# A decoder layer on one core: the token sums' tiles start at another byte, and the first round of the gates spreads its seven products over more units

## The chip, the cores and the metric

The kernel runs on one core of a Trainium2 chip. The metric is the time of one launch on the device in microseconds (us); lower is better. A profile is one execution taken by the hardware profiler, and its trace can be asked for every instruction.

Engines are called by the profile's names: PE multiplies matrices (PEld is its loading of the stationary operand), DVE, ACT and POOL work on vectors, SP issues most of the transfers from memory.

## The reference, cut to what matters

One layer of a hybrid decoder works on 272 tokens (16 meta tokens and 256 others) of width 2048, all in float32:

```
proj = rmsnorm(h) @ w_in                 # one combined input projection
o_fox = forgetting_attention(...)        # 8 heads of 128
o_gla = gated_linear_attention(...)      # 4 heads, keys of 256, values of 512
y = sigmoid(gate_fox) * (o_fox @ w_o_fox) + sigmoid(gate_gla) * (o_gla @ w_o_gla)
h = h + y @ w_out
h = h + square(relu(rmsnorm(h) @ w_ff1)) @ w_ff2      # inner width 8192
out = rmsnorm(h)[:, 16:]
```

What bears on this case are the two gates' projections (`gate_fox`, `gate_gla`, each 2048 by 2048) with the branches' output projections, and the two matrices of the last sublayer.

## The kernel before, in words

**Precision.** A float32 operand is cut into two parts of a shorter type: ACT casts it to the high part (line 991 in `cut`), DVE subtracts that from the original to get the low part (line 992). A product of two cut operands is three matmuls on PE: high by high, high by low, low by high (`product_into`, line 1005). The stationary operand is a block of 128 by 128 numbers of the activations (tokens by inner dimension), the moving operand a row of 512 weights, so each of these matmuls streams 512 columns.

**Units.** A weight transfer of 512 KB fills a tile `raw` (five buffers), its cut fills a tile `w` (five buffers) that holds two blocks of the inner dimension for 512 columns. One such unit feeds twelve matmuls: two halves of the tokens (t = 0, 1), two blocks, three parts.

**Pairs with seven products.** The gates and the last sublayer are computed by `pair_of`: two column blocks f1 and f2 at a time, both token halves. For the first four blocks of the inner dimension it does not do the eight products of a 2 by 2 block product but seven (a scheme of Strassen's kind). For that it needs sums and differences of weights, which DVE makes from `hb`, `hc` and the raw tiles (line 996, `less`), and sums of token blocks, made once for each operand by `token_sums`. Four of the seven products take such a sum as the stationary operand (`summed(0)` to `summed(3)`). The seven products are step1 to step7; `held`, ahead of them, only issues the transfers of `hb` and `hc`. Step1 ends with a copy of bank x to bank y on ACT (line 1050), step2 with a copy of bank v to `m5` (line 1057). Step3 ends with z = x + m5 on DVE (line 1063), step4 with v = x + m5 (line 1067): the banks x, y, z, v are accumulators, so step4's product into x has to come behind the first of these additions, and any other product into x behind the second. The other twelve blocks of the inner dimension follow as plain units (six for each of the two column blocks).

**The rounds.** `columns` (heading of the code below: the function that the second part of the change touches) runs three rounds of the gates' pairs (b = 0, 1, 2). The list `work` has 24 units a round: eight `lone` units of the GLA branch's projection (tiles `gla<-w,og`), twelve plain units of the gates' pair (`bx`, `by`, `bz`, `bv` with `x` as the other operand), four `lone` units of the FoX branch's projection (`fox<-w,of`). A table `at` says behind which unit each of `held` and step1 to step7 is put. In the last sublayer thirteen pairs follow each other in the same way, seven with the operand x2 and six with the operand a, by a table of their own at the program's end; the four products with sums of each pair take their stationary operand from the tiles `s_x2` and `s_a`. (The profile leaves buffer numbers out of names: `x2` reads as `x` and `s_x2` as `s_x` there. Before 776 us `s_x` is the gates' own tile of sums, later it is `s_x2`.)

A scheduler that works on an estimated timeline places the instructions of each engine, so an instruction can end up some places before or behind where the code has it. `tc.keep_in_program_order` fixes `less` in its place.

**Where the operands begin.** Tiles of cut operands carry some spare columns, so that the code can choose the byte at which the operand begins (`at=24`, `at=56`, `SX_AT`, `SUMS_AT`; units of four bytes). The addresses in a partition, as the built program has them:

| operand | used as | in | begins at byte | past a multiple of 64 | past a multiple of 256 |
|---|---|---|---|---|---|
| x (cut activations), og, of | stationary | gates | 36992, 74112, 178304 | 0 | 128 |
| s_x (sums for the gates) | stationary | gates | 19328 | 0 | 128 |
| w in the gates' rounds | moving | gates | 128704 and on | 0 | 192 |
| x2, a | stationary | last sublayer | 73984, 37120 | 0 | 0 |
| s_x2, s_a, before | stationary | last sublayer | 197920, 206368 | 32 | 32 |
| s_x2, s_a, after | stationary | last sublayer | 197888, 206336 | 0 | 0 |
| w in the last sublayer's pairs | moving | last sublayer | 128576 and on | 0 | 64 |

Blocks inside an operand lie whole multiples of 256 bytes apart.

Of the kernel before, what the change touches and what calls it, by code (L numbers as in the profile page):

```python
# [30 lines left out]
BIG = 3.0e38  # L31
RAW = 5
NL = 4
SUMS_AT = 32
SX_AT = 0
PARTS_AT = 56

# [36 lines left out]
def trunk(ctx: ExitStack, tc: tile.TileContext, hT, w_small, w_all, consts, w_alpha2, out):  # L74
# [3 lines left out]
    def nm(s):  # L78
        serial[0] += 1
        return f"{s}_{serial[0]}"  # L80
# [11 lines left out]
    def bank(pool, s):  # L92
        return pool.tile([P, 512], F32, tag="bank", name=nm(s))
# [7 lines left out]
    def issued():  # L101
        for e in list(waiting):
            e[0] -= 1
            if e[0] <= 0:
                waiting.remove(e)
                e[1]()
# [126 lines left out]
    def cells(ap):  # L233
        return ap.rearrange("p (j m) -> p j m", m=P)

    def turn(rows, then, both, far=None, slots=(10, 12, 14), reload=None):

        n = 4 * NT
        for t, r in enumerate(rows):
            nc.vector.transpose(both[:, 0:n].rearrange("p (i t j r) -> p t i j r", i=4, t=2, r=32)[:, t],  # L240
                                r().rearrange("p j (i s) -> p i j s", i=4, s=32))
        there = far or dram.tile([P, n], F32, tag="there", name=nm("there"), bufs=2)

        def away():
            for c in range(4):
                nc.scalar.dma_start(there.rearrange("(i s) (c e) -> c s i e", i=4, c=4)[c],
                                    both[32 * c : 32 * c + 32, 0:n].rearrange("s (i e) -> s i e", i=4))

        behind.append([slots[0], away])
        if reload:  # L250
            behind.append([slots[0], reload])
        if far is None:
            back = both[:, n:]
            behind.append([slots[1], lambda: nc.scalar.dma_start(back, there)])
            behind.append([slots[2], lambda: then(returned(back))])
# [717 lines left out]
    def fetched(c0, k0, hold=None, pairs=False):  # L973
        if hold:
            raw = hold_pool[0].tile([P, HK * P], F32, tag=hold, name=nm(hold))
        else:
            raw = wp.tile([P, HK * P], F32, tag="raw", name=nm("raw"), bufs=RAW)
        cols = slice(k0 * P, (k0 + 2) * P)
        if pairs:
            for c in range(2):  # L980
                nc.sync.dma_start(raw[:, HK * P // 2 * c : HK * P // 2 * (c + 1)].rearrange("p (h e) -> p h e", h=2),
                                  w_all[c0 + c].rearrange("p (h e) -> p h e", h=2)[:, :, cols])
            return raw
        nc.sync.dma_start(raw.rearrange("p (c k m) -> p c k m", k=2, m=P),
                          w_all[c0 : c0 + 4, :, cols].rearrange("c p (k m) -> p c k m", m=P))
        return raw

    def cut(raw, low=False):
        hi, lo = (t.rearrange("p k m -> p (k m)").rearrange("p (k c m) -> p k c m", k=2, m=P) for t in pair(low=low))
        r = raw.rearrange("p (c k m) -> p k c m", k=2, m=P)  # L990
        copied = nc.scalar.copy(hi, r).ins  # L991
        made(copied, nc.vector.tensor_tensor(lo, r, hi.bitcast(F32), op=ALU.subtract).ins, 1)  # L992
        return [t.rearrange("p k c m -> p k (c m)") for t in (hi, lo)]
# [6 lines left out]
    def product_into(ps, xs, w, start=False):  # L1000
        for k in range(2):
            hi, lo = w[0][:, k, :], w[1][:, k, :]
            xh, xl = xs(k, 0), xs(k, 1)
            for i, (l, r) in enumerate(((xh, hi), (xh, lo), (xl, hi))):
                nc.tensor.matmul(steps(ps), l, steps(r), start=start and k == 0 and i == 0, stop=False,  # L1005
                                 skip_group_check=True)

    def tokens(x, t, k0):
        return lambda k, o: x[:, k0 + k, o, P * t : P * t + P]
# [89 lines left out]
    def columns():  # L1099

        hold_pool[0] = mp
        waiting_rows, far, made_s = {}, [], {}

        def lone(b, which, k0):
            key = (which, b)
            if k0 == 0:
                waiting_rows[key] = [bank(pg if which == "gla" else px, which), bank(px, which)]
            src, c0 = (og, A0 + 14 * b) if which == "gla" else (of, A0 + 14 * b + 12)
            w = cut(fetched(c0, k0, pairs=which == "fox"), True)
            for t, ps in enumerate(waiting_rows[key]):  # L1110
                product_into(ps, tokens(src, t, k0), w, k0 == 0)
            if which == "fox" and k0 == 6:
                joined(b)

        def gated(b, f, pt):
            g = "gf"[f]
            u = made_s[b, g] = mp.tile([P, 2, 512], F32, tag="s" + g, name=nm("s" + g))
            for t, ps in enumerate(pt):
                nc.scalar.activation(u[:, t, :], ps, AF.Sigmoid, scale=r1[:, t : t + 1])
            if g == "g":  # L1120
                for t, ps in enumerate(waiting_rows["gla", b]):
                    nc.vector.tensor_tensor(u[:, t, :], ps, u[:, t, :], op=ALU.mult)

        def joined(b):
            sf, sg = made_s[b, "f"], made_s[b, "g"]
            for t, ps in enumerate(waiting_rows["fox", b]):
                nc.vector.tensor_tensor(sf[:, t, :], ps, sf[:, t, :], op=ALU.mult)
            for t in range(2):
                nc.vector.tensor_tensor(sf[:, t, :], sf[:, t, :], sg[:, t, :], op=ALU.add)
            far.append(dram.tile([P, 4 * NT], F32, tag="far", name=nm("far"), bufs=3))  # L1130
            turn([lambda t=t: cells(sf[:, t, :]) for t in range(2)], None, sg.rearrange("p t f -> p (t f)"),
                 far=far[b], slots=(8,))

        made_pairs = [pair_of(A0 + 14 * b + 4, x, s_x, lambda f, pt, b=b: gated(b, f, pt), True, low=True)
                      for b in range(3)]
        work = []
        for b in range(3):
            work += [lambda b=b, k=k: lone(b, "gla", k) for k in range(0, KT, 2)]
            work += made_pairs[b][1]
            work += [lambda b=b, k=k: lone(b, "fox", k) for k in range(0, KT // 2, 2)]  # L1140
        at = {}
        for n, i in enumerate((-1, 0, 2, 3, 4, 5, 6, 7)):
            at.setdefault(i, []).append(made_pairs[0][0][n])
        for b in (1, 2):
            for n, i in enumerate((-3, -2, 0, 2, 3, 4, 6, 7)):
                at.setdefault(24 * b + i, []).append(made_pairs[b][0][n])
        for run in at[-1]:
            run()
        for i, run in enumerate(work):
            run()  # L1150
            for step in at.get(i, []):
                step()
            issued()
        chunk[0] += 42
        backs = [mp.tile([P, 4 * NT], F32, tag=t, name=nm("back")) for t in ("ha", "hb", "hc")]
        for b in (0, 1):
            nc.scalar.dma_start(backs[b], far[b])
        behind.append([11, lambda: nc.scalar.dma_start(backs[2], far[2])])
        return backs

    backs = columns()
    residual[0] = keep.tile([P, KT, NA + 3], F32, tag="h", name="h2")

# [49 lines left out]
    def sums_tile(name):  # L1213
        t = fp.tile([P, 16 * P + 64], F32R, name=name)
        return t[:, SUMS_AT : SUMS_AT + 16 * P].rearrange("p (s k o m) -> p s k o m", k=2, o=2, m=P)

# [325 lines left out]
```

## Time and profile before

| | |
|---|---|
| Median of 3 runs | 1517.83 us (1517.62 to 1518.39) |
| The profiled execution | 1518.05 us |
| its span, first to last instruction | 1516.3 us |
| granted TensorE clock | 0.999 |
| PE busy | 1505.9 us (99%) |
| DVE busy | 1121.8 us (74%) |
| ACT busy | 852.1 us (56%) |
| gates' rounds (matmuls of line 1005) | 482 to 700 us |
| output projection | about 740 to 841 us |
| last sublayer's pairs | 841 to 1377 us, their first products with sums from 784 us on |
| products of the last pair in token rows (lines 224 to 226) | 1377 to 1398 us |

How to read it: matmuls are pipelined, each is shown with a duration of about 380 ns although the next begins after 220 ns, so that PE reads as busy almost always. What a matmul costs is the distance from its beginning to the next one's. The chain of waits shows that: it lists pieces in order of time with the time that each took from the end of the piece before it, and a piece of x12 over 2.64 us is twelve matmuls 220 ns apart. A row of a view by windows gives the count of instructions that touch the window, so it counts one that began ahead of its left edge.

### The profile page before, as it was taken

The page shows a single profiled execution, that of the slowest core. Times are in us where ns is not written, and L with a number is a line of the kernel's source. Part 1 is how long each engine was busy: PE and PEld are TensorE (multiplying, and loading weights), DVE is VectorE, ACT ScalarE, POOL GpSimd, SP SyncE. Part 2 cuts the span into 40 slices and gives each one's busy share as a digit, 9 for nine tenths or more (in the row PEclk, how much of TensorE's full clock was granted, in tenths as well). Part 3 has the DMA queues.
Part 4 walks back from the last instruction along what each step waited for, and adds up shares of the span by engine and source line. Part 5 has one row for each costly group of instructions (what it writes and reads, how often), then busy time and mean ns, then how long its engine had stood idle before and what let it go on. Part 6 is the DMA issues. An engine that isn't in the chain of part 4 may idle for free.

```text
span 1516.3 us, 22651 instructions
## 1 busy us (share of the span) xinstructions
PE 1505.9 (99%) x8518; PEld 1334.7 (88%) x8518; DVE 1121.8 (74%) x1508; ACT 852.1 (56%) x1223; POOL 129.5 (9%) x200
## 2 busy tenths in 40 slices
PE   9999999999999999999999999999999999999997
PEld 8999999999998888888988888888888888888997
DVE  7898858586676766756798887677877788875765
ACT  7766444555555554444566666556654566455563
POOL 6012110111111000000011000000000000100021
PEclk9999999999999999999999999999999999999999
DMA  9545545465555757586668588567775678787652
GB/s 319 177 146 187 178 159 192 156 211 174 169 185 182 230 185 236 184 291 212 217 212 263 168 282 258 196 198 249 251 236 196 214 244 259 250 292 253 228 201 86
DMA packets 224194, 323.10 MB, mean 213 GB/s; under 512 B 12154, under 2 KB 189316, under 8 KB 223956
## 3 DMA queue, kind: packets, MB, share of 16 engines
q1 hardware_dynamic: 203332, 292.40, 58.5%
q10 hardware_dynamic: 20496, 27.99, 6.0%
q8 instruction: 67, 1.10, 0.3%
q0 software_dynamic: 256, 1.26, 0.3%
q14 instruction: 43, 0.35, 0.1%
HBM read 305.86 MB, written 15.74 MB: 212 GB/s over the span
## 4 chain that ended last, share of the span: by engine, by line
PE 96%; DVE 2%; issue 1%; ACT 1%; POOL 0%; POOLq 0%; DVEq 0%
PE ps L191 16%; PE bx L1005 14%; PE bz L1005 10%; PE by L1005 10%; PE bv L1005 10%; PE ps L192 8%; PE psa L196 5%; PE psa L200 5%; PE psa L198 4%; PE gla L1005 4%; PE fox L1005 2%; PE ps L466 2%; PE ps L468 1%; PE ps L1409 1%; DVE w L135 1%
## 5 line engine op out<-in xcount | busy, mean ns | idle before, releaser
L992 DVE TENSOR_TENSOR w<-raw,w 128x1024 fp32r<-128x1024 f32 x260 | 319.8, 1231 | 152.7 <-ACT w L991 148.4
L991 ACT CAST w<-raw 128x1024 fp32r<-128x1024 f32 x260 | 271.3, 1048 | 218.6 <-PE bv L1005 86.2
L135 DVE TENSOR_TENSOR w<-raw,w 128x1024 fp32r<-128x1024 f32 x222 | 272.5, 1228 | 101.4 <-ACT w L134 97.8
L134 ACT CAST w<-raw 128x1024 fp32r<-128x1024 f32 x222 | 232.6, 1049 | 97.0 <-PE psa L200 30.7
L191 PE MATMUL ps<-x,w 128*128 128x512 f32 x607 | 206.0, 383 | 0.0
L196 PE MATMUL psa<-x,w 128*128 128x272 f32 x640 | 181.7, 285 | 0.0
L200 PE MATMUL psa<-x,w 128*128 128x272 f32 x640 | 179.7, 282 | 0.0
L198 PE MATMUL psa<-x,w 128*128 128x272 f32 x624 | 175.9, 282 | 0.0
L192 PE MATMUL ps<-x,w 128*128 128x256 f32 x607 | 166.6, 274 | 0.0
L191 PEld LDWEIGHTS ps<-x,w 128*128 128x128 f32 x607 | 113.9, 188 | 19.3
L196 PEld LDWEIGHTS psa<-x,w 128*128 128x128 f32 x640 | 120.2, 188 | 0.2
L200 PEld LDWEIGHTS psa<-x,w 128*128 128x128 f32 x640 | 120.2, 188 | 0.1
L1005 PE MATMUL bx<-w,x 128*128 128x512 f32 x480 | 120.1, 382 | 0.0
L198 PEld LDWEIGHTS psa<-x,w 128*128 128x128 f32 x624 | 117.4, 188 | 0.0
L192 PEld LDWEIGHTS ps<-x,w 128*128 128x128 f32 x607 | 114.0, 188 | 0.0
L1005 PE MATMUL by<-w,x 128*128 128x512 f32 x420 | 105.8, 382 | 0.0
L1005 PEld LDWEIGHTS bx<-w,x 128*128 128x128 f32 x480 | 89.8, 187 | 16.6
L1005 PE MATMUL bv<-w,x 128*128 128x512 f32 x360 | 91.6, 383 | 0.0
L1005 PEld LDWEIGHTS by<-w,x 128*128 128x128 f32 x420 | 78.7, 187 | 14.5
L1005 PE MATMUL bz<-w,x 128*128 128x512 f32 x360 | 91.4, 383 | 0.0
L191 PE MATMUL ps<-y,w 128*128 128x512 f32 x256 | 85.7, 380 | 0.0
L991 ACT CAST w<-ha 128x1024 fp32r<-128x1024 f32 x48 | 50.3, 1047 | 53.2 <-PE bx L1005 22.7
(405 smaller groups left out, 2776.1 us busy)
## 6 DMA issues: line engine op xcount, KB each, us to landing
raw<-w_all_dram SPq DMA_DIRECT2D x493, 512.0 KB, 4.3
there<-turn ACTq DMA_DIRECT2D x76, 128.0 KB, 4.2
turn<-there ACTq DMA_DIRECT2D x19, 512.0 KB, 5.5
hb<-w_all_dram SPq DMA_DIRECT2D x16, 512.0 KB, 4.3
hc<-w_all_dram SPq DMA_DIRECT2D x16, 512.0 KB, 5.9
raw<-w_all_dram SPq DMA_DIRECT2D x26, 256.0 KB, 3.4
raw<-w_all_dram SPq DMA_DIRECT2D x8, 384.0 KB, 6.5
h<-hT_dram SPq DMA_DIRECT2D x8, 275.0 KB, 6.8
```

Source lines behind the costliest of these rows:

```text
L134: copied = nc.scalar.copy(hi[:, k, :], r).ins
L135: return copied, nc.vector.tensor_tensor(lo[:, k, :], r, hi[:, k, :].bitcast(F32), op=ALU.subtract).ins
L191: nc.tensor.matmul(steps(ps), hi, steps(row(x)), start=first, stop=False)
L192: nc.tensor.matmul(steps(ps[:, 0:NT]), lo, steps(x[:, 0, :]), start=False, stop=last)
L196: nc.tensor.matmul(steps(ps[:, X_LO]), hi, steps(x_lo[:, k]), start=first, stop=False, skip_group_check=True)
L198: nc.tensor.matmul(steps(ps[:, 0:NA]), lo, steps(x_hi[:, k]), start=False, stop=last and hi is None, skip_group_check=True)
L200: nc.tensor.matmul(steps(ps[:, 0:NA]), hi, steps(x_hi[:, k]), start=False, stop=last, skip_group_check=True)
L466: nc.tensor.matmul(steps(ps), hi, steps(row(x[:, k])), start=st, stop=False)
L468: nc.tensor.matmul(steps(ps[:, 0:NT]), lo, steps(x[:, k, 0]), start=False, stop=sp)
L991: copied = nc.scalar.copy(hi, r).ins
L992: made(copied, nc.vector.tensor_tensor(lo, r, hi.bitcast(F32), op=ALU.subtract).ins, 1)
L1005: nc.tensor.matmul(steps(ps), l, steps(r), start=start and k == 0 and i == 0, stop=False, skip_group_check=True)
```

## The change

Two numbers change. The constant `SUMS_AT`, the place at which the sums' operand begins in the tiles `s_x2` and `s_a`, goes from 32 to 24 (32 bytes further to the front). And the table for the first round (b = 0) in `columns` is spread out: `held` stays ahead of the first unit, step1 to step7 come behind units 1, 3, 5, 7, 9, 10 and 12 instead of 0 and 2 to 7.

```
-SUMS_AT = 32
+SUMS_AT = 24
...
         at = {}
-        for n, i in enumerate((-1, 0, 2, 3, 4, 5, 6, 7)):
+        for n, i in enumerate((-1, 1, 3, 5, 7, 9, 10, 12)):
             at.setdefault(i, []).append(made_pairs[0][0][n])
```

The first number moves no instruction. The second does, in the first round alone. On PE, at the round's beginning, this stood before (gla and og are the GLA branch's accumulators and input, bx and bv the gates' accumulators, w a cut weight tile):

```order
L1005 MATMUL gla_5833<-w_5837,og_1382 128x4x32x4 x6
L1005 MATMUL gla_5834<-w_5837,og_1382 128x4x32x4 x6
L1005 MATMUL bx_5859<-w_5854,x 128x4x32x4 x6
L1005 MATMUL gla_5833<-w_5870,og_1382 128x4x32x4 x6
L1005 MATMUL gla_5834<-w_5870,og_1382 128x4x32x4 x6
L1005 MATMUL gla_5833<-w_5887,og_1382 128x4x32x4 x6
L1005 MATMUL gla_5834<-w_5887,og_1382 128x4x32x4 x6
L1005 MATMUL bv_5906<-w_5902,s_x 128x4x32x4 x6
```

and now stands this:

```order
L1005 MATMUL gla_5833<-w_5837,og_1382 128x4x32x4 x6
L1005 MATMUL gla_5834<-w_5837,og_1382 128x4x32x4 x6
L1005 MATMUL gla_5833<-w_5854,og_1382 128x4x32x4 x6
L1005 MATMUL gla_5834<-w_5854,og_1382 128x4x32x4 x6
L1005 MATMUL bx_5876<-w_5871,x 128x4x32x4 x6
L1005 MATMUL gla_5833<-w_5887,og_1382 128x4x32x4 x6
L1005 MATMUL gla_5834<-w_5887,og_1382 128x4x32x4 x6
L1005 MATMUL gla_5833<-w_5904,og_1382 128x4x32x4 x6
L1005 MATMUL gla_5834<-w_5904,og_1382 128x4x32x4 x6
L1005 MATMUL bv_5923<-w_5919,s_x 128x4x32x4 x6
```

Step1 (bx from x) and step2 (bv from s_x) each stand one or two GLA units later.

Where step4 and step5 stood on PE among the last GLA units (bx and bz from s_x), before:

```order
L1005 MATMUL gla_5833<-w_5999,og_1382 128x4x32x4
L1005 MATMUL gla_5834<-w_5999,og_1382 128x4x32x4
L1005 MATMUL bx_5859<-w_5961,s_x 128x4x32x4 x6
L1005 MATMUL bz_5942<-w_5988,s_x 128x4x32x4 x6
L1005 MATMUL gla_5833<-w_5999,og_1382 128x4x32x4 x5
L1005 MATMUL gla_5834<-w_5999,og_1382 128x4x32x4 x5
L1005 MATMUL by_5866<-w_6016,x 128x4x32x4 x6
```

they now stand among the first plain units (by and bx from x):

```order
L1005 MATMUL gla_5834<-w_5997,og_1382 128x4x32x4 x6
L1005 MATMUL by_5883<-w_6024,x 128x4x32x4 x3
L1005 MATMUL bx_5876<-w_6012,s_x 128x4x32x4 x6
L1005 MATMUL by_5883<-w_6024,x 128x4x32x4 x3
L1005 MATMUL by_5883<-w_6041,x 128x4x32x4 x6
L1005 MATMUL bz_5976<-w_6056,s_x 128x4x32x4 x6
L1005 MATMUL by_5883<-w_6067,x 128x4x32x4 x6
L1005 MATMUL bx_5876<-w_6024,x 128x4x32x4 x6
L1005 MATMUL bx_5876<-w_6041,x 128x4x32x4 x6
```

The scheduler has put the plain products into bx of three units behind three units' products into by, because the addition of step4 stands between them. On DVE, the two additions (lines 1063 and 1067) stood before among these cuts:

```order
L992 TENSOR_TENSOR w_5988<-hc_5831,w_5988 128x1024
L1063 TENSOR_TENSOR bz_5942<-bx_5859,m_821_5913 128x512
L992 TENSOR_TENSOR w_5999<-raw_5997,w_5999 128x1024
L992 TENSOR_TENSOR w_6016<-raw_6014,w_6016 128x1024
L996 TENSOR_TENSOR ha_5857<-raw_6014,ha_5857 128x1024
L992 TENSOR_TENSOR w_6028<-raw_6026,w_6028 128x1024
L1067 TENSOR_TENSOR bv_5906<-bx_5859,m_821_5913 128x512
L992 TENSOR_TENSOR w_6043<-ha_5857,w_6043 128x1024
```

and now among these:

```order
L992 TENSOR_TENSOR w_6024<-raw_6022,w_6024 128x1024
L1063 TENSOR_TENSOR bz_5976<-bx_5876,m_823_5930 128x512
L992 TENSOR_TENSOR w_6041<-raw_6039,w_6041 128x1024
L992 TENSOR_TENSOR w_6056<-hc_5831,w_6056 128x1024
L992 TENSOR_TENSOR w_6067<-raw_6065,w_6067 128x1024
L1067 TENSOR_TENSOR bv_5923<-bx_5876,m_823_5930 128x512
L992 TENSOR_TENSOR w_6084<-raw_6082,w_6084 128x1024
L996 TENSOR_TENSOR ha_5874<-raw_6082,ha_5874 128x1024
L992 TENSOR_TENSOR w_6096<-raw_6094,w_6096 128x1024
```

The first addition now stands behind the cut of the first plain unit, the second behind two more. Also on DVE, at the round's beginning, the first difference of weights (line 996, from `hb`) comes one place earlier: ahead of the eviction of the last gate of the stage before (line 287) and of the cut of `w_5904`, where it stood behind that eviction. On SP the transfers of the second round's `hb` and `hc` are issued some places later among those of the raw tiles. POOL's order is the same.

## The prediction

> **What bounds the kernel now.** I read the page first: its busy times and its chain of waits.
>
> ```profile
> span 1516.3 us, 22651 instructions
> PE 1505.9 (99%) x8518; PEld 1334.7 (88%) x8518; DVE 1121.8 (74%) x1508; ACT 852.1 (56%) x1223; POOL 129.5 (9%) x200
> PE 96%; DVE 2%; issue 1%; ACT 1%; POOL 0%; POOLq 0%; DVEq 0%
> ```
>
> PE is the bound from one end to the other. So the question for each half of the change is not who is busy, but whether PE waits anywhere that the change touches, and how far apart its matmuls begin. I therefore went to the chain in order of time, which gives that distance. First the gates' rounds, with pieces that take the sums as stationary operand (491.59) and pieces that don't:
>
> ```profile
> 482.35 2.64 PE gla L1005 x12
> 491.59 1.32 PE bv L1005 x6
> 544.39 7.92 PE fox L1005 x36
> ```
>
> Each is 0.220 us a matmul: 2.64/12, 1.32/6, 7.92/36. Now the last sublayer, from its first pair on:
>
> ```profile
> 841.73 1.32 PE bx L1005 x6
> 849.65 1.76 PE bx L1005 x8
> 855.38 0.89 PE by L1005 x4
> 856.27 1.35 PE bv L1005 x6
> 858.07 2.69 PE bx L1005 x12
> 894.38 2.68 PE bx L1005 x12
> 975.48 2.74 PE bx L1005 x12
> ```
>
> It also begins at 0.220 (1.32/6, 1.76/8). At 856.27 come six products with the sums `s_x2`: 0.225 each. After them the distance doesn't go back, although the operands are again x2 and plain weights: 0.223 at 894 (2.68/12), 0.228 at 975 (2.74/12). Over whole stages (PE's rows by windows; the gates' rounds, the pairs from the first sums at 856 on, and the last pair's token rows):
>
> ```profile
> 482.35:699.90 217.55, 217.55 (x991) 1.00 0.69 225
> 856.11:1376.98 520.87, 520.87 (x2319) 1.00 0.75 239
> 1376.98:1398.20 21.22, 21.22 (x96) 1.00 0.78 264
> ```
>
> The clock is 1.00 in all three. 217.55 us at 0.220 is 989 matmuls, which is the count but for the edge and two short ones at the left: no time is lost in the gates. 520.87 us for 2318 (one of the 2319 began earlier) is 0.2247 each: the last sublayer's pairs are 2% slower than the same instruction in the gates. That is not a wait for another engine, as PE's rows there show no idle time, and it is not the work beside it, since it begins with one group of products. The same group can be watched where it stands alone among the output projection's matmuls (512 and 256 columns in turn):
>
> ```profile
> 803.82 0.38 PE L191 MATMUL ps<-y,w 128*128 128x512 f32 x1
> 804.15 1.51 PE L1005 MATMUL bx<-w,s_x 128*128 128x512 f32 x6
> 805.51 0.38 PE L191 MATMUL ps<-y,w 128*128 128x512 f32 x1
> 806.86 0.38 PE L191 MATMUL ps<-y,w 128*128 128x512 f32 x1
> 808.19 0.38 PE L191 MATMUL ps<-y,w 128*128 128x512 f32 x1
> ```
>
> From 804.15 to 805.51 the six with sums take 1.36 us where six take 1.32 in the gates; the four pairs from 805.51 take 1.35, the next four 1.33. The disturbance comes with the sums and dies out here; among the pairs of the last sublayer it stays.
>
> **What sets the sums apart.** All stationary operands of the pairs, x2 and a, and all of the gates, begin at a multiple of 64 bytes; `s_x2` and `s_a` alone begin 32 bytes past one. The gates' own sums begin at a multiple and run at 0.220. So my theory is: while a matmul streams its moving operand, PE loads the next stationary block; these two streams run in step as long as their offsets agree, the 32 bytes put them out of step, and x2 and a can't bring them back.
>
> **Part one, SUMS_AT 32 to 24.** It adds and removes no instruction. After it `s_x2` and `s_a` begin at a multiple of 64, in fact of 256, as x2 and a do. If the step is kept, each of the 2318 matmuls costs what x2's cost at 841 to 850: 2318 x 0.220 = 510.0, against 520.87: -10.9 us. The last pair's token rows (95 that begin in the window, 0.2234 each) follow in the same state: 95 x 0.220 = 20.9 against 21.22, -0.3. The four groups with sums ahead of 856, of which the one at 804 is quoted, lose 1.36 - 1.32 = 0.04 each and 0.02 behind it: -0.2 in all. Sum -11.4. No row in these stages is below 0.220, so that is also the most that it can give.
>
> The least: only the sums' own products improve and x2 and a stay at the 0.2233 of the row at 894. Then 2318 x 0.2233 = 517.6: -3.2 us (less the token rows, which are there already). Below nothing: everything settles at the 0.2283 of the row at 975, 2318 x 0.2283 = 529.2, +8.4. I take the first value: x2 has run at 0.220 with exactly the addresses that all operands will have, and 72 products with aligned sums in the gates have not moved their neighbours.
>
> A rule speaks against this half. The Trainium skill, page "SBUF — State Buffer", section "Who interferes with whom", gives PE two independent read ports, one for the moving operand and one for the weight load, and says that PE never waits on anyone; by that rule the start byte would change nothing and part one would come to 0. The trace doesn't bear it out: the products at 856.27 and 491.59 differ in nothing that the profile shows but their operands, and take 1.35 and 1.32.
>
> Does another engine become late when PE is 2% faster? DVE is the nearest (columns: PE, PEld, DVE, ACT, POOL):
>
> ```profile
> 482.00:545.00 63.00, 63.00 (x289) 53.75 (x288) 41.01 (x37) 32.28 (x35) 0.73 (x1) 1.00 0.71 227
> 866.80:945.00 78.20, 78.20 (x351) 65.44 (x350) 64.42 (x66) 50.07 (x60) 0.00 (x0) 1.00 0.84 267
> ```
>
> In the densest stretch it works 64.4 of 78.2 us, 82%; with 1.5 to 2% less time, 84%. The stretch at 856 and on has PE without idle time at 82%, so I put this at 0, with 0.5 us as the bound for a few first waits.
>
> **Part two, the first round's table.** It moves step1 to step7 behind later units; the same matmuls, cuts, differences and transfers are issued. What it could remove is PE's waiting in that round, up to its first FoX product:
>
> ```profile
> 482.35:544.39 62.04, 62.04 (x284) 1.00 0.71 227
> ```
>
> There is none: 282 matmuls (two of the 284 began earlier) at 0.220 are 62.04. So its gain is bounded at 0. What it could add hangs on three places.
>
> ```profile
> L1063 DVE TENSOR_TENSOR bz<-bx,m 128x512 f32<-128x512 f32 x16 | 11.1, 694 | 3.1 <-PE bx L1005 3.1
> L1067 DVE TENSOR_TENSOR bv<-bx,m 128x512 f32<-128x512 f32 x16 | 11.1, 694 | 1.7 <-PE bx L1005 1.7
> L992 DVE TENSOR_TENSOR w<-raw,w 128x1024 fp32r<-128x1024 f32 x260 | 319.8, 1231 | 152.7 <-ACT w L991 148.4
> L991 ACT CAST w<-raw 128x1024 fp32r<-128x1024 f32 x260 | 271.3, 1048 | 218.6 <-PE bv L1005 86.2
> L287 DVE TENSOR_TENSOR evt<-ps,evb 128x256 f32<-128x256 f32 x5 | 2.1, 423 | 2.1 <-ACT evb L284 2.1
> L996 DVE TENSOR_TENSOR ha<-hb,raw 128x1024 f32<-128x1024 f32 x1 | 1.2, 1226 | 1.3 <-DMA hb<-w_all_dram 1.3
> ```
>
> First, step4's product into x must wait for step3's addition (0.69 us). Between the two on PE lie two GLA units and three products of a plain one, 27 x 0.22 = 5.9 us, and DVE's cuts for these are made ahead, since five tiles are in turn. Covered. Second, the plain products into bx wait for step4's addition, 0.69 us; the scheduler has put 21 products = 4.6 us between, and behind the addition on DVE queues the cut of `w_6084`, which PE needs only 39 products = 8.6 us after step4. The tightest cut behind is that of `w_6096`: its buffer is that of `w_6024`, free when PE has done that tile's six products into bx, and its turn comes 18 products = 4.0 us later, against 1.05 + 1.23 = 2.3 us for cast and subtraction. Covered by 1.7 us. Third, the first difference now stands on DVE ahead of an eviction and of the cut of `w_5904`. It waits for `hb` to land; the view of that tile gives its start:
>
> ```profile
> L996 DVE TENSOR_TENSOR ha<-hb,raw x1: 1226/1226/1226, 484.6 to 484.6; 128x1024 f32<-128x1024 f32 x1
>   DMA hb<-w_all_dram: 1.3, 1
> ```
>
> From 484.6, difference, eviction and cut end at 484.6 + 1.23 + 0.42 + 1.23 = 487.5; PE gets to `w_5904` after 42 products, 482.35 + 9.24 = 491.6. Covered by 4.1 us. The second round's `hb` and `hc` go behind a few raw tiles on SP and are needed from about 552 on. I take 0 for the part; if one cover were wrong, the price is one cast and cut late, 2.3 us.
>
> **The sum.** -10.9 - 0.3 - 0.2 + 0 = -11.4, less up to 0.5 for waits that I can't see: about -11.2. The profiled execution took 1518.05, its span 1516.3; the median of the runs, 1517.83, is 0.2 lower. 1517.83 - 11.2 = 1506.6.
>
> **Rivals.** What 0.2% is, 3.0 us, is about what a measurement of this kernel can tell from no change.
>
> *The after-effect stays* (chance 0.13). The sums run clean, but something else (the first matmuls of a stage, a short wait) puts x2 and a out of step, and they stay at 0.2233. For it: nearly all of x2's matmuls run so, for tens of us at a time without a product of sums between. Against: they don't until the first sums come, 841 to 856, two groups with a break at 851 for the norm's own matmuls included. Price: -3.2, so 1514.6, or anything between that and the forecast if it sets in late.
>
> *The start byte doesn't matter* (0.07). The distance of 0.225 would come from the sums in some other way, such as the accumulators' bank. Then neither half does anything: 1517.8. Against: the gates go through the same seven steps at 0.220. The Trainium skill's rule on PE's two read ports, above, would have it come out so.
>
> *Slower: the whole stage locks in the slow step* (0.04). The row at 975 shows that a step of 0.2283 can hold over dozens of matmuls with aligned operands. If the new start byte puts the streams into that one at the first sums, the pairs cost 529.2: +8.4, so 1526. It decides for slower once more than about a half of the stage runs so, with the rest at 0.2233. Against: now it follows only where two groups of sums stand close together at the odd offset.
>
> **The numbers.** The forecast has 0.76. Its own range is 1505.8 to 1508.5 (all terms, with up to 2 us of a wait). To leave no more than 2 in 10 out the range takes in late cases of the first rival, up to 1512. Faster by over 0.2% means under 1514.8: the forecast and most of the first rival, 0.85. Within 0.2%: the rest of it and the second, 0.11. Slower: 0.04.
>
> **What would show it.** After the change the chain should have 2.64 for every x12 and 1.32 for every x6 between 856 and the pairs' end, which comes at about 1366; the token rows 2.64 for twelve. The gates' first round should still be 62.0 us for its 282. I am wrong in the mechanism if a group with sums still takes 1.35; in its after-effect if sums take 1.32 and x2 2.68; in part two if PE has idle time between 482 and 545.

## The result, and the profile after

| | median | runs | ratio to before (95%) |
|---|---|---|---|
| before, on the same chip | 1518.14 us | 6 | |
| after | 1507.91 us (1507.29 to 1508.06) | 6 | 0.9933 (0.992 to 0.9945) |

The change makes the kernel 10.2 us faster; 11.2 had been forecast. The profiled execution of after has a span of 1506.3 us, 10.0 less than that of before.

The page of after, its span, busy times and the chain by engine:

```profile
span 1506.3 us, 22650 instructions
PE 1494.7 (99%) x8518; PEld 1335.2 (89%) x8518; DVE 1120.5 (74%) x1508; ACT 851.2 (57%) x1223; POOL 128.4 (9%) x200
PE 95%; DVE 2%; issue 1%; ACT 1%; DMA 0%; SPq 0%; POOL 0%; POOLq 0%; DVEq 0%
```

PE does the same 8518 matmuls and is the bound as before; its busy time has changed by 11.2 us, no other engine's by more than 1.3. Where that went, the chain of waits in after shows at the places where the prediction read it in before (start, time, engine, accumulator, count):

```profile
842.66 1.33 PE bx L1005 x6
850.69 1.79 PE bx L1005 x8
852.60 0.89 PE bx L1005 x4
853.93 0.34 PE pn L1286 x3
857.35 1.32 PE bv L1005 x6
859.11 2.64 PE bx L1005 x12
894.75 2.64 PE bx L1005 x12
```

The six products with sums take 1.32 (857.35; 1.35 before), and x2's keep 2.64 for twelve behind them (2.69 and 2.68 before). But the head of the stage is new: from 842.66 to 850.69 x2's products begin 0.2233 apart (1.79/8), where they had 0.220 before, and go back to 0.220 behind the norm's own matmuls (`pn`).

The stages, PE's rows by windows: the gates' first round, the pairs from the first sums on, the last pair's token rows:

```profile
482.66:544.70 62.04, 62.04 (x284) 1.00 0.64 213
857.19:1367.15 509.96, 509.96 (x2320) 1.00 0.76 244
1367.15:1388.27 21.12, 21.12 (x97) 1.00 0.81 266
```

The pairs' 2318 matmuls take 509.96 us, 0.220 each. (The window's edges follow the matmuls' own starts, which lie some 0.16 us ahead of the chain's pieces.) The gates' first round is what it was, to the hundredth.

What lies between is the output projection, where the y matmuls (512 and 256 columns in turn, tile `ps`) have single groups of pair products among them. After, in the chain:

```profile
799.25 1.33 PE bx L1005 x6
...
804.66 1.33 PE bx L1005 x6
806.00 0.23 PE ps L191
...
808.38 0.23 PE ps L191
```

and before:

```profile
798.94 1.35 PE bx L1005 x6
...
804.32 1.35 PE bx L1005 x6
805.67 0.22 PE ps L191
...
808.35 0.22 PE ps L191
```

Before, the group itself was slow (1.35), and eight pairs of y matmuls behind it take 2.68 us (805.67 to 808.35), 0.335 each, and soon 0.333 again, as the prediction saw. After, the group is quicker, but the pairs behind it take 0.34 each and don't recover: seven of them 2.38 us (806.00 to 808.38), and so on to the projection's end. From 799.25 to 842.66 that is 43.41 us, against 42.79 before (798.94 to 841.73): +0.62. The slow head of x2's products, 842.66 to 857.35, is 14.69 against 14.54: +0.15.

So the spans' difference adds up: +0.31 (there already at 482.66 against 482.35, ahead of all that changed, and still at 799), +0.62, +0.15, -10.91 in the pairs, -0.3 in the token rows (after has 96 in 21.12, the prediction's row of before 95 in 21.22), and about +0.1 at the end: -10.0.

### The profile page after: what moved, and what is told of

Read it like the earlier page. It is cut to its first block, busy times and chain, and to the rows that moved or that the text cites. A ratio compares the mean times of both kernels' runs of the same rounds, so it can differ in the third digit from the quotient of the medians.

```text
span 1506.3 us, 22650 instructions
## 1 busy us (share of the span) xinstructions
PE 1494.7 (99%) x8518; PEld 1335.2 (89%) x8518; DVE 1120.5 (74%) x1508; ACT 851.2 (57%) x1223; POOL 128.4 (9%) x200
## 4 chain that ended last, share of the span: by engine, by line
PE 95%; DVE 2%; issue 1%; ACT 1%; DMA 0%; SPq 0%; POOL 0%; POOLq 0%; DVEq 0%
PE ps L191 16%; PE bx L1005 14%; PE by L1005 10%; PE bv L1005 10%; PE bz L1005 10%; PE ps L192 8%; PE psa L196 5%; PE psa L200 5%; PE psa L198 4%; PE gla L1005 4%; PE fox L1005 2%; PE ps L466 1%; PE ps L1409 1%; PE ps L468 1%; DVE w L135 1%
## 5 line engine op out<-in xcount | busy, mean ns | idle before, releaser
L1005 PEld LDWEIGHTS bz<-w,x 128*128 128x128 f32 x360 | 67.6, 188 | 11.6
```

## The experiments

A word for what the addresses of one matmul and the next give: the **lead** is the byte at which the next stationary operand begins less the byte at which the running matmul's moving operand begins, modulo 256. By the addresses in the built programs it is 192 nearly everywhere in this kernel: in the gates 128 - 192, in the pairs with x2 and a 0 - 64, in the output projection 64 - 128 (weights stationary there, y moving). Before the change the sums had 32 - 64, so 224.

### The two parts alone

```
e1_sums_only: before, with
-SUMS_AT = 32
+SUMS_AT = 24
e2_table_only: before, with
-        for n, i in enumerate((-1, 0, 2, 3, 4, 5, 6, 7)):
+        for n, i in enumerate((-1, 1, 3, 5, 7, 9, 10, 12)):
```

> The sums begin 32 bytes further to the front, the first round's table is the old one. My theory puts the whole gain on the sums: the chain shows 2.64 us for twelve matmuls in the last sublayer's pairs, the time is that of the changed kernel, 1507.9 within 0.5. The rival, that the spread table has a part in the gain (or has taken some of it back), would have it off by more than 1 us.

> The spread table alone, the sums at their old byte. My theory: nothing, 1518.1 within 0.5, since PE waits nowhere in that round before or after. The rival that spreading the products saves or costs something there: off by 1 us or more.

Measured: the sums alone 1507.44 us (5 runs), ratio 0.9932 (0.9919 to 0.9944); the table alone 1517.95 (11 runs), ratio 1.0001 (0.9992 to 1.001). All of the gain is the 32 bytes; the table does nothing that can be measured.

### Is a multiple of 64 enough?

The prediction's theory was that operands at multiples of 64 bytes run in step. These two put the sums at 64 and at 128 past a multiple of 256 (lead 0 and 64).

```
e3_sums_64: after, with
-SUMS_AT = 24
+SUMS_AT = 40
e4_sums_128: after, with
-SUMS_AT = 24
+SUMS_AT = 56
```

> The changed kernel with the sums 64 bytes past a multiple of 256 (SUMS_AT 40): still a multiple of 64 bytes, but the distance from the moving operand's first byte to the next stationary operand's, taken modulo 256, is 0 for the sums where it is 192 for x2 and a. As I predicted it, a multiple of 64 is enough: 1507.9, 0.220 us a matmul. The rival, that this distance must be the same for all operands: products with sums slower than 0.220 again, x2 and a put out of step behind them, 1514 to 1522.

> The changed kernel with the sums 128 bytes past a multiple of 256 (SUMS_AT 56), the distance from moving to next stationary operand 64 modulo 256, the same as that of x2 and a modulo 128. If a multiple of 64 is enough, or the distance counts modulo 128: 1507.9. If it counts modulo 256: out of step behind each group of sums, 1514 to 1522.

Measured: 1516.11 (10 runs), ratio 0.9989 (0.998 to 0.9998), and 1513.98 (10 runs), ratio 0.9976 (0.9967 to 0.9985). With the sums at 64, the chain:

```profile
894.04 2.68 PE bx L1005 x12
900.08 1.35 PE bv L1005 x6
1140.26 2.64 PE bx L1005 x12
1147.10 1.37 PE bv L1005 x6
```

and with the sums at 128:

```profile
893.93 2.68 PE bx L1005 x12
899.95 1.39 PE bv L1005 x6
904.70 1.32 PE bz L1005 x6
```

Both have slow groups with sums (1.35 to 1.39 us), x2 and a sometimes at 0.220 and mostly at 0.2233. So a multiple of 64 isn't enough, nor is one of 128: the theory as I had put it is too wide. What counts goes by at least 256 bytes, and of the four places tried the sums are quick only where they begin as x2 and a do.

### Is it the lead, and is the lead's change at an edge what slows the output projection?

At the edges of a group among the y matmuls the lead changes in after: the pair's weights begin at 64 and the y weights behind them at 64, lead 0; y begins at 128 and the pair's operand at 0, lead 128. Four kernels, all after with an edit:

```
e5_y_48: y 128 bytes further (lead 64 in all of the projection)
-    y = operand(keep, "y", at=16, tag="s1")
+    y = operand(keep, "y", at=48, tag="s1")
e6_all_32: x2, a and the sums all 32 bytes further (lead 224 in all pairs)
-SUMS_AT = 24
+SUMS_AT = 32
-    x2 = operand(keep, "x2", at=24, tag="s2")
+    x2 = operand(keep, "x2", at=32, tag="s2")
-            a_box[g] = operand(keep, "a", at=48, tag="s1")
+            a_box[g] = operand(keep, "a", at=56, tag="s1")
e7_w_192: the pairs' weights at 192, as in the gates (lead 64 in all pairs)
-            return cut(raw, low)
+            return cut(raw, True)
e8_y_edge: y at 64 and its weights at 0: lead 192 in the projection and at both edges
-        a, b = (0, 20) if meta else (56, 56) if low else (24, 24)
+        a, b = (0, 20) if meta else (8, 8) if low == "y" else (56, 56) if low else (24, 24)
-    y = operand(keep, "y", at=16, tag="s1")
+    y = operand(keep, "y", at=0, tag="s1")
-        add_residual(j, gemm2(next_weights(), y))
+        add_residual(j, gemm2(next_weights(low="y"), y))
```

> The changed kernel with the output projection's input y at a multiple of 256 instead of 128 past it: the distance from moving to next stationary operand is 64 (modulo 256) all through that projection, where it was 192; the pairs keep 192. If a constant distance is enough, the projection's pairs of 512 and 256 columns settle at 333 ns as before the change and the time is 1507 to 1508. If the distance has to be 192, they run at 340 ns or more all through: 144 pairs more than now, about 1 us and up to 3 us slower, 1509 to 1511.

> The changed kernel with x2, a and both tiles of sums all 32 bytes past a multiple of 256: the distance is 224 (modulo 256) for all pairs of the last sublayer, constant, but not a multiple of 64. If only a constant distance counts: 0.220 us a matmul, 1507.9 within 1. If it has to be 192: every matmul of the pairs at 0.2245 or more (what the sums took before the change), 2400 x 4.5 ns = 11 us slower, 1518 or more.

> The changed kernel with the cut weights of the last sublayer's pairs 192 past a multiple of 256, not 64: the distance is 64 (modulo 256) for x2, a and the sums alike. Constant distance is enough: 0.220 us a matmul in the pairs, 1507.9 within 1. It has to be 192: 1513 to 1520, with the pairs at 0.2225 or more. It shows by itself that the place of the moving operand counts as much as that of the stationary one, if the time moves.

> The changed kernel with y 64 past a multiple of 256 and the output projection's weights at a multiple of 256: the distance is 192 inside that projection as now, and 192 too where its matmuls and the pairs' first products follow each other (now 0 and 128). My theory of the 0.8 us that the change lost there (340 ns a pair behind each group of products, where 333 are the step): they come back, the pairs of the projection stay at 333 ns and x2's first groups at 0.220, 0.6 to 0.9 us faster than the changed kernel. If the loss has another cause: as the changed kernel.

Measured:

| kernel | lead | runs | ratio (95%) |
|---|---|---|---|
| e5_y_48 | 64 in the projection | 1506.96 to 1507.58 (4) | 0.9932 (0.9919 to 0.9945) |
| e6_all_32 | 224 in the pairs | 1520.26; 1507.97 to 1508.39 (4) | 0.9938 (0.9924 to 0.9952) |
| e7_w_192 | 64 in the pairs | 1521.92 to 1523.27 (5) | 1.0031 (1.0019 to 1.0043) |
| e8_y_edge | 192 also at the edges | 1513.36, 1525.05; 1505.69 to 1506.90 (10) | 0.9939 (0.9919 to 0.9959) |

PE's row for 857 to 1366 counts how many of the pairs' matmuls begin in 509 us. It reads, in e7_w_192:

```profile
857.00:1366.00 509.00, 509.00 (x2247) 1.00 0.76 235
```

With the one that began earlier left out that is 509.00/2246 = 0.2266 us each: the pairs are slower than in before (0.2247) although the lead never changes. So one lead throughout isn't enough; which one it is counts, and the place of the other operand, the weights, counts too.

Nor is 192 the only lead that can be quick. Four of the five executions of e6_all_32 took 1508.0 to 1508.4 us, as was expected if a constant lead is enough. The fifth, the profiled one, ran most of its pairs at 0.2252 (below) and took 1520.26; 2090 matmuls at 0.0052 more would be 11 us, for which the four have no room. That their pairs ran at 0.220 is worked out so, not seen. The lead 224, slow in before, where the sums alone had it among operands at 192, is then not slow in itself.

e5_y_48, with the lead 64 in the output projection, is neither slower nor faster than after: 358 matmuls between 780 and 842 us, where after has 357. Its pairs of y matmuls settle at 0.335 and 0.338 in turn, so neither at the 0.333 nor at the 0.340 that had been expected.

In e8_y_edge the output projection keeps its pace, as wanted; the row for 780 to 842 in it, in after and in e7_w_192:

```profile
780.00:842.00 62.00, 62.00 (x361) 1.00 0.74 230
```

```profile
780.00:842.00 62.00, 62.00 (x357) 1.00 0.70 226
```

```profile
780.00:842.00 62.00, 62.00 (x361) 1.00 0.72 227
```

Four more matmuls in the same time than in after (the two sizes together are 0.333, so 0.7 us), and ten of twelve executions take 1505.7 to 1506.9, where after's take 1507.3 to 1508.1 (in the median 11.6 us under before on its chip, against after's 10.2). That fits an edge as what slows the projection in after. But it is not a rule that an edge needs the lead 192: e7_w_192, with 128 at both edges, has slow groups of pair products there (1.35 to 1.36 us for six), and its y matmuls still go back to 0.333 behind each. And the profiled execution of e8_y_edge was not one of these, and shows something else. Its chain, and the load of a stationary block at 898 (in the timeline; in brackets the idle time before it and who ended it):

```profile
892.44 2.64 PE bx L1005 x12
897.94 0.23 PE bx L1005
898.17 0.50 PE by L1005
898.67 1.34 PE bv L1005 x6
912.74 2.68 PE bz L1005 x12
```

```profile
898.17 0.19 PEld L1005 LDWEIGHTS by<-w,x 128*128 128x128 f32 x1 [0.42 <-DVE w L992]
```

Up to 898 all is at 0.220. There PE waits once for a cut on DVE, one matmul takes 0.50 us instead of 0.22, and behind it the matmuls of the stage are 0.2233 apart on average, with the same instructions and addresses. In e6_all_32's profiled execution (the one of 1520.26) it turns at the same place (the chain, the loads just ahead of the turn, and PE's row for the rest of the stage):

```profile
894.13 2.64 PE bx L1005 x12
900.08 1.35 PE bv L1005 x6
```

```profile
899.25 0.19 PEld L1005 LDWEIGHTS bx<-w,x 128*128 128x128 f32 x1
899.58 0.19 PEld L1005 LDWEIGHTS by<-w,x 128*128 128x128 f32 x1
```

```profile
925.00:1366.00 441.00, 441.00 (x1959) 1.00 0.74 234
```

Ahead of the turn a load begins every 0.22 us, together with a matmul; the one at 899.58 comes 0.1 us late. DVE's last cut before it began at 898.30 and took 1.22 us, so it ended 0.06 us ahead of that load, where in e8_y_edge the load followed 0.05 us behind its cut. No matmul is late here, and yet the rest runs at 441.00/1958 = 0.2252. The profile names no releaser for a delay this short; that the load waited for this cut is read from the two times.

So a kernel's addresses don't fix its pace: there are at least two paces that last, and something at 898 to 900 can turn the one into the other. The suspect was the wait for the cut, as the products with sums of a begin there and DVE makes these sums shortly before.

### Does a wait of PE turn the pace?

e9_turn_early takes the wait away from e8_y_edge: the first turn of every pair that makes sums of a is started one unit earlier, so that DVE is done earlier. e10 and e12 make DVE late in the changed kernel, with no address changed, by making the first sums of a twice or four times (the same numbers again). e11_norm_late moves the norm's four matmuls, behind which after had gone back to 0.220.

```
e9_turn_early: e8_y_edge, with
-  ... (7, 11, 14) if p + f == 0 else (7, 11, 15),
+  ... (6, 10, 13) if p + f == 0 else (7, 11, 15),
e10_sums_twice (in e12_sums_four: 4 for 2): after, with
             if summed:
-                token_sums(s_a, ...)
+                for _ in range(2 if len(a_box) == 1 else 1):
+                    token_sums(s_a, ...)
e11_norm_late: after, with
-            if index == 0 and i == 2:
+            if index == 0 and i == 4:
                 norm2()
```

> The kernel of the run with y at 0 and its weights moved, and one number set changed: the first turn of each pair with the operand a goes away, comes back and is summed one unit earlier. In that earlier run PE waited 0.4 us at 898 for a cut on DVE, which was late behind the sums of a, and went on at 223.3 ns instead of 220 to the end (1513.4); two of its twelve executions were above 1513, ten at 1505.7 to 1506.9. Theory: one wait of PE in the pairs can throw the two streams into the slow pace, and nothing else was slow there. Then with the sums a unit (2.6 us) earlier there is no wait at 898, 220 ns holds to 1366, and all executions lie at 1505.5 to 1507. Rival: the slow pace comes by chance or by that kernel's other addresses; then about one execution in six is again above 1513, with or without a wait.

> The changed kernel, with the sums of a for the first of the pairs that use it made twice (same numbers): 3 to 4 us more on DVE near 895 to 900, where PE has 1.6 us in hand; all addresses as they are. Theory: PE then waits some 1 to 3 us at about 900, and behind that wait its pace can be 0.2233 or 0.225 with the same addresses, for hundreds of us: 2090 matmuls x 0.0033 = 7 us, so executions at about 1509 to 1511 (pace kept) and about 1516 to 1518 (pace lost), perhaps both. Rival: the pace follows from the addresses alone, and a wait costs itself only: all executions at 1509 to 1511, with 220 ns behind the wait.

> The changed kernel with the second norm's own four matmuls put two units later (behind unit 4 of the first pair, not 2). In the changed kernel x2's products run at 223.3 ns from 842.5 on, when the output projection ends in the slow pace, and at 220 from the norm's matmuls at 852 on. Theory: these four matmuls, with other operands, bring the streams back into step. Then the slow pace lasts about 5 us longer here and ends again right behind them: 0.1 us in time, to be read in the trace alone. Rival: it ends by itself after some 10 us, or with the next sums; then it ends at about 852 to 857 with the norm's matmuls behind.

> The changed kernel with the sums of a for the first of the pairs that use it made four times (same numbers, same addresses), about 10 us more on DVE from 893 on. With the sums made twice, seven of twelve executions took 1514.5 to 1527.5 and five 1507.3 to 1507.9, but the one that was profiled was of the five and had no wait of PE. Theory: the slow executions are those in which PE waits for a cut on DVE somewhere behind the sums and comes out of step there. With four times the work the profile should show such a wait (some 2 to 5 us at 900 to 915) and behind it x6 pieces of 1.34 or 1.38 us to the end: 1507.5 + 2 to 5 + 7 or 19, so 1516 to 1531, or 1509 to 1513 where the wait leaves PE in step. Rival: the slow pace has nothing to do with waits: then 1.32 us for every x6 behind the wait, and slow executions no more frequent than in the changed kernel, where none of six was slow.

Measured:

| kernel | runs | ratio (95%) |
|---|---|---|
| e9_turn_early | 1505.92 to 1506.39 (5) | 0.9923 (0.9911 to 0.9935) |
| e10_sums_twice | 1507.33 to 1507.88 (5); 1514.45 to 1515.64 (4); 1517.45; 1527.35, 1527.47 | 0.9981 (0.9955 to 1.0007) |
| e11_norm_late | 1507.76 (1) | |
| e12_sums_four | 1513.62, 1513.97; 1518.76 to 1521.88 (6); 1531.20 | 1.0017 (0.9992 to 1.0042) |

e9_turn_early, chain and the row from 857 to the end of its pairs:

```profile
898.43 1.10 PE by L1005 x5
899.53 1.32 PE bv L1005 x6
```

```profile
857.00:1364.00 507.00, 507.00 (x2306) 1.00 0.76 244
```

There is no wait at 898 and 0.220 holds to the end (507.00/2305). It is 11.5 us under before on its chip, as quick as the ten quick executions of e8_y_edge (11.6). That none of five executions was slow proves little by itself: with two of twelve slow, five quick ones in a row would come four times in ten.

e12_sums_four shows that a late DVE alone, with after's addresses, can bring the slow pace about. PE's rows ahead of the place, at it and behind it, and two of the loads that waited:

```profile
857.00:893.00 36.00, 36.00 (x165) 1.00 0.88 258
893.00:925.00 32.00, 28.32 (x123) 1.00 0.59 191
925.00:1366.00 441.00, 441.00 (x1976) 1.00 0.75 239
```

```profile
912.68 0.98 PEld L1005 LDWEIGHTS bz<-w,x 128*128 128x128 f32 x5 [1.31 <-DVE w L992]
...
917.71 0.74 PEld L1005 LDWEIGHTS bv<-w,s_a 128*128 128x128 f32 x4 [0.52 <-DVE s_a L292]
```

Ahead of the waits 0.220 (36.00/164), as in after; behind them 441.00/1975 = 0.2233, to the end. The waits themselves cost 32.00 - 122 x 0.220 = 5.2 us, the pace behind them 1975 x 0.0033 = 6.5; together 11.7, and this execution took 1519.47, 11.6 over after's median. The two quick executions, 5.7 and 6.1 us over after, are what the waits alone make; they have no profile, so that their pace stayed at 0.220 is worked out, not seen.

e10_sums_twice gave less than it was made for: its profiled execution had no wait (the scheduler put the products with `s_a` behind others), and took 1507.38, with 0.220 throughout. Its other executions lie above the first group by about 7 us (four), 10 (one) and 20 (two). For the 2095 matmuls behind 905, 7 and 20 us would be 0.2233 and 0.2295, estimates without a profile; the slowest row of before had 0.2283. Five of twelve stayed quick, where none of six of after's was slow. Whether each slow one had a wait isn't shown.

e11_norm_late went against what I expected of it (its chain, and the loads ahead of the turn):

```profile
859.14 0.47 PE pn L1286 x4
859.61 1.36 PE bx L1005 x6
894.47 2.68 PE bx L1005 x12
900.28 0.22 PE by L1005
900.50 1.32 PE bv L1005 x6
```

```profile
899.67 0.19 PEld L1005 LDWEIGHTS bx<-w,x 128*128 128x128 f32 x1
899.99 0.19 PEld L1005 LDWEIGHTS by<-w,x 128*128 128x128 f32 x1
```

The norm's matmuls, here four in one piece, don't bring 0.220 back. It stays at 0.2233 for 41 us more and turns to 0.220 with the first products of `s_a` at 900. No matmul is late there, but the load at 899.99 is, by 0.1 us, 0.05 behind the end of DVE's cut (898.72 and 1.22 us long): the same late load as in e6_all_32, and here it turns the slow pace into the quick one. In after the norm's four matmuls stand as one and three with six others between. So a break can turn the pace in either direction or leave it, and I have no rule for which.

Over all fourteen profiled executions, the loads between 857 and 1364 us begin within 0.01 us of a matmul's beginning, but for those that come late in e6_all_32, e8_y_edge, e11_norm_late and e12_sums_four. In these four the pace turns just there; after, e1, e5, e9 and e10 have no late load and stay at 0.220 all through, and e7_w_192 has none and stays at 0.2266. Where the sums have another lead than x2 and a (before, e2, e3, e4), the pace also changes at their groups, with no late load.

## Why the prediction was right, and where it was not

**Part one, 2318 x 0.220 (-10.9).** Right: 509.96 us, -10.91, and the table and the sums alone give that all of it is the 32 bytes.

**The token rows (-0.3).** Right: 21.12 us for the 96, 0.220 each, as the state at the pairs' end is kept.

**The early groups with sums (-0.2).** Wrong in sign and size: the output projection is 0.62 slower and x2's first products 0.15. I looked at the group itself, which did become quicker, and took for granted that nothing behind it is worse than before. The step that failed is "x2 has run at 0.220 with exactly the addresses that all operands will have": true inside a stage, but a group also has two edges, and there the operands' places change (lead 0 and 128). By chance the y matmuls went back to 0.333 a few pairs behind the slow group of before, and don't behind the quick one of after. With another place for y and its weights (e8_y_edge, e9_turn_early) the projection is quick again; which leads at an edge do harm stays open. This term, 1.0 us off, is most of the 1.2 us between forecast and spans.

**Part two (0).** Right: 62.04 us for the first round's 282 matmuls in both, and 1.0001 for the table alone. The three covers held, as there is no wait.

**No other engine late (0 to 0.5).** Right for after: 509.96 leaves no room for a wait. But the reserve was smaller than I had it: in e8_y_edge, with PE a little further ahead, it waits for DVE's cut at 898 (its products get there 2.0 us earlier than after's, the cuts on DVE only 0.4). I had bounded such a wait by its own length. Its price can be the pace behind it, 7 us for 0.3 us of wait.

**The theory.** Half right. Paces that last, a start byte that sets them off, and x2 and a going on in the pace that they are left in: that is what the runs show. That these are two streams of PE in step or out of step is not shown: at 0.220 and at 0.2233 alike each load begins with a matmul, within 0.01 us. The "multiple of 64" is wrong: 64 and 128 past a multiple of 256 are slow for the sums. The forecast held all the same because 24 puts the sums where x2 and a begin, modulo 256, which the prediction had also gone by. And the start byte alone doesn't decide: e12_sums_four runs at both paces with after's addresses.

**The rivals.** *The after-effect stays* was priced as if it had one cause, the sums. It is real and lasts (1513.4 in e8_y_edge, 1519.5 in e12_sums_four), but in after's pairs it shows for the 10 us behind 842.66 only. *The start byte doesn't matter* fell: 1507.44 with the sums moved and nothing else, 10.4 us under before on the same chip. The Trainium skill's rule in the page "SBUF — State Buffer", section "Who interferes with whom", that PE's two read ports are independent, would have given 0 here; the runs give 10.4 us for 32 bytes of the operand that is loaded. *Slower* has its place too, though not here: e7_w_192 locks at 0.2266 and is slower than before.

## What to carry to other kernels

Where matmuls stand back to back, compare their start-to-start distance between stages with the same shape; a difference of one or two per cent at full clock, without idle time, is worth trying the start bytes of both operands for, modulo 256, and a place where the kernel already runs at the better pace shows which to take. Look at the edges between groups and not only inside them. And do not let PE wait even once in a stage that has the better pace: here 0.3 us of wait could cost 7 us behind it, and in e6_all_32 a load 0.1 us late, which held up no matmul, went with 12 (1520.3 against 1508.2), so that the last microsecond of reserve on the engine that feeds it is worth more than it seems.

## What the runs showed of the hardware

- The same matmuls (512 columns, granted clock 1.00) begin 0.220, 0.2233 or 0.2252 to 0.2283 us apart, and a pace can last for hundreds of microseconds: 1975 matmuls at 0.2233 in e12_sums_four.
- With the sums 32, 64 or 128 bytes from where x2 and a begin (modulo 256) their groups of six take 1.35 to 1.39 us instead of 1.32. With all operands at one lead of 64 the pairs run at 0.2266, with one of 224 at 0.220 up to 900 us and at 0.2252 behind it in the one profiled execution. A lead of 192 is the only one at which a profile shows 0.220 over the whole stage; with 224, four executions of 1508.0 to 1508.4 us leave no room for anything else.
- A load that waits for a cut can turn the quick pace into a slow one (0.4 us of idle load time at 898 in e8_y_edge; 5.2 us of waits in all in e12_sums_four; a load 0.1 us late, with no matmul late, in e6_all_32) or the slow into the quick (0.1 us late in e11_norm_late). Other breaks turn it back (the norm's matmuls at 852 in after) or don't (the same four at 859 in e11_norm_late).
- What is open: the mechanism behind the paces. That the load of the next stationary block and the stream of the moving operand meet in the memory is the reading that fits the addresses; no run here shows it.
